# Dilated-window softmax heads on one core: the scores of four heads as one issue unit, values as the stationary operand in column halves, output kept feature-major

## The chip, the cores and the metric

The kernel runs on one core of one Trainium2 chip. The metric is the device time of one execution in microseconds (us), a median over runs; lower is better. The two engines that this document mostly speaks of are TensorE (rows named PE for its matmuls, PEld for the loads of its stationary operand) and the engines that feed it: VectorE (DVE), ScalarE (ACT) and the DMA queue of SyncE (SP).

## The reference

A two-layer decoder trunk on 512 tokens of 1024 features. Layer 0 mixes tokens with four gated delta-rule heads and eight dilated sliding-window softmax heads, layer 1 with a state-space mixer; each is followed by cross-attention and a feed-forward block. The change touches the eight softmax heads alone. Each of three branches attends, from query t, the keys t, t-r, t-2r, ... back to t-window, and the branches are weighted by their log-sum-exp:

```python
SW_BRANCHES = ((128, 1), (512, 4), (2048, 16))
...
    scores = jnp.einsum('brnqhd,brnkhd->brnhqk', qb, kw,
                        preferred_element_type=jnp.float32) * (d ** -0.5)
...
    p = jnp.exp(scores - m)
    l = p.sum(-1)
    o = jnp.einsum('brnhqk,brnkhd->brnqhd', p, vw.astype(jnp.float32))
    o = o / jnp.swapaxes(l, -1, -2)[..., None]
...
    wts = jax.nn.softmax(jnp.stack(lses), axis=0)[..., None]
    return jnp.sum(jnp.stack(outs) * wts, axis=0)
```

With 512 tokens this is one softmax per query over all earlier keys, with the logarithm of the number of branches that see a key (0 to 3) added to its score. The kernel computes it in that form: an additive mask `attm` holds 8 times that logarithm, or -1e30.

## The kernel before

**An order by recording.** The program does not issue instructions as it is written. Class `Order` records every engine call as an operation (`add`, line 219), gives it an estimated duration (`cost`, line 187), and `order` (line 270) then simulates the engines: each engine takes the first operation in program order whose operands are there and whose buffers are free. `issue` (line 417) emits the result; every instruction therefore carries line 422 in the profile, and groups are told apart by tile names and shapes. Tile names: `ps` is a PSUM bank (8 of them), `t` a 128x512 scratch tile in SBUF (13), `big` a 128x2048 tile (16), `raw`, `hi`, `lo` the weights as fetched and split into two parts of reduced float32, `ident` the identity for transposes.

**Products.** Large projections run as three matmuls in reduced float32 (hi*hi, hi*lo, lo*hi; one matmul record each). The softmax heads use plain float32; there one matmul of the program shows as two records, each with its own weight load.

**The softmax heads** are the end of `mixer0` (lines 986 to 1017). Queries and keys lie feature-major, two heads of 64 features in the 128 partitions of `qkT`, values token-major in `Vt`. For each block `i` of 128 queries and each of 8 heads, with n = (i+1)*128 keys:

1. scores: a matmul of 64 rows (a head's features) by n columns into a bank of its own (line 994); even heads lie in partitions 0 to 63, odd heads in 64 to 127;
2. DVE adds the mask and takes the row maximum (line 997), scales it (998); ACT takes the exponential and its row sums (999);
3. PE transposes the weights, i+1 blocks of 128x128 (line 1000); DVE (even heads) or ACT (odd heads) copies them to SBUF (1002 to 1005);
4. the product with the values (line 1007): i+1 matmuls whose stationary operand is the transposed weights (128 columns) and whose moving operand is 64 columns of `Vt`; the output is token-major, 64 columns of the bank `ov` per head.

After the 8 heads the block is scaled by the reciprocal sums on DVE (1014), transposed by PE to feature-major and split into hi and lo parts by ACT and DVE (`to_mix`, line 885), as the operand of the output projection. After each pair of heads the program draws one step of `fill`, the key projection of the cross-attention (`mem_k`, 256-column products). What follows is that output projection (`mix_out0`, 512-column products): the half of its contraction that reads the delta-rule heads can run before the softmax heads are done, the other half cannot.

Of the kernel before, what the change touches and what calls it, by code (L numbers as in the profile page):

```python
# [12 lines left out]
AF = mybir.ActivationFunctionType  # L13
OP = mybir.AluOpType
AX = mybir.AxisListType

P = 128
# [75 lines left out]
class Engine:  # L93
    """Records the calls of an engine instead of issuing them."""
# [10 lines left out]
class Order:  # L105
    """The order in which the recorded instructions are issued: for each engine, the first in program
    order of those whose operands are there, by estimates of what the instructions take."""
# [12 lines left out]
    def either(self, *calls):  # L120
        """The same result by one of several engines: (engine, function, args, kwargs)"""
        self.add(list(calls))

# [6 lines left out]
    # ---- what an access touches  # L130
# [40 lines left out]
    @staticmethod  # L171
    def operands(fn, args, kw):
# [14 lines left out]
    def cost(self, eng, fn, outs, ins, kw):  # L187
        o = outs[0]
        n = 1
        for _, c in list(o.ap)[1:]:  # L190
            n *= c
        psum = any("PSUM" in str(x.space) for x in ins)
# [25 lines left out]
    # ---- recording  # L218
# [50 lines left out]
    # ---- ordering  # L269
# [147 lines left out]
    def issue(self):  # L417
        seq, prio = self.ops, [op.prio for op in self.ops]
        self.issued = self.order(seq, prio)
        with self.tc.manual_schedule():  # L420
            for op, (e, fn, args, kw, _) in self.issued:
                op.inst = getattr(self.eng[e], fn)(*args, **kw)  # L422
# [21 lines left out]
class Trunk:  # L444
# [32 lines left out]
    def weights(self, w, k0, n, c0, width):  # L477
        """n row tiles of w by `width` columns as high and low parts, fetched ahead of the program"""
# [93 lines left out]
    def transposes(self, src, n, width=P):  # L572
        """n blocks of [128, width] from src to one bank [width, n, 128]"""
# [9 lines left out]
    def mixer0(self, fill):  # L583
# [6 lines left out]
        # ---- x, transposed  # L590
# [14 lines left out]
        # ---- constants  # L605
# [19 lines left out]
        # ---- rotary tables  # L625
# [14 lines left out]
        # ---- beta and decay logits, feature-major then token-major  # L640
# [57 lines left out]
        # ---- delta-net q, k, v  # L698
# [44 lines left out]
        # ---- the decay inside a chunk, [j, (head, i)]  # L743
# [24 lines left out]
        # ---- chunk matrices, [j, (head, i)]: L^T above its diagonal  # L768
# [25 lines left out]
        # ---- q and v  # L794
# [3 lines left out]
        # ---- inverse of the 32 x 32 diagonal blocks, one system a partition (h, c, b)  # L798
# [17 lines left out]
        # ---- the products of q and k under the decay  # L816
# [12 lines left out]
        # ---- the gate of the delta-net heads  # L829
# [8 lines left out]
        # ---- merge the blocks: X' = X - X E X for 32, 64  # L838
# [41 lines left out]
        # ---- sequential part over chunks  # L880
# [80 lines left out]
        # ---- the sliding-window heads  # L961
# [24 lines left out]
        off = 0  # L986
        for i in range(NT):
# [3 lines left out]
            for h in range(8):  # L991
                rs = slice(64 * (h % 2), 64 * (h % 2) + 64)
                sp = self.bank()
                T.matmul(sp[:, :n], qkT[0][rs, h // 2, i * P:(i + 1) * P], qkT[1][rs, h // 2, :n], start=True, stop=True)
                pm = t2()
                mx = tiny(1)
                V.tensor_tensor_reduce(pm[:, :n], sp[:, :n], attm[:, off:off + n], 1.0, NEG, OP.add, OP.max, mx)
                V.tensor_scalar(mx, mx, -0.125, None, op0=OP.mult)
# [10 lines left out]
                if h % 2:  # L1009
                    next(fill, None)  # L1010
# [657 lines left out]
```

## Time and profile before

| | |
|---|---|
| median of 3 runs | 1574.64 us |
| lowest and highest run | 1571.55, 1580.14 us |
| span of the profiled execution | 1572.0 us |
| PE busy | 1539.2 us, 98% of the span |
| PEld busy | 1300.8 us, 83% |
| DVE busy | 990.3 us, 63% |
| ACT busy | 550.9 us, 35% |
| DMA | 184.06 MB, mean 117 GB/s |

The profiled execution has no separate time of its own besides its span of 1572.0 us, which lies between the lowest and the median run; nothing measurable lies around it. The softmax heads take the stretch from about 235 to 316 us, with the key projection and the output projection mixed into it. The mean granted clock of TensorE over the span is 0.994. In the rows, "busy" is the union of the records' intervals; matmul records are pipelined and overlap, so a duration of a matmul record is longer than what it costs. What a piece of PE work costs is read from the distance between the starts of two pieces.

### The profile page before, as it was taken

The numbers are of one execution on the slowest core, as the hardware profiler recorded it, in microseconds if no ns is written. First come the engines' busy times: TensorE is split into PE (matmuls) and PEld (weight loads), VectorE is DVE, ScalarE is ACT, GpSimd is POOL, SyncE is SP. The second block draws the span as 40 slices with busy tenths as digits, with TensorE's granted clock in tenths as the row PEclk, the third lists the DMA queues.
The fourth block names the chain that finished last, engine by engine and source line by source line (L and its number), as shares of the span: only waits on it lengthen the run. The fifth ranks groups of instructions, "written<-read, shape, count | busy, mean of one in ns | idle before, by whom it ended". The sixth has DMA issues, their size and how long they took to land.

```text
span 1572.0 us, 20938 instructions
## 1 busy us (share of the span) xinstructions
PE 1539.2 (98%) x8132; PEld 1300.8 (83%) x8132; DVE 990.3 (63%) x1890; ACT 550.9 (35%) x988; POOL 58.2 (4%) x97
## 2 busy tenths in 40 slices
PE   7999999999999999999999899999999999999998
PEld 5887878778988888888888798888888888888886
DVE  6989666556557788725754899748657443334436
ACT  6533436424432344423441233332422322222211
POOL 1100000000000000010000000000000000000000
PEclk9999999999999999999999999999999999999999
DMA  6423224125314344526572554323213333233322
GB/s 184 125 60 95 81 89 134 51 71 168 91 37 132 111 166 163 183 84 201 188 254 81 201 176 148 125 94 108 88 37 98 107 102 100 73 115 96 105 68 94
DMA packets 125539, 184.06 MB, mean 117 GB/s; under 512 B 14144, under 2 KB 84800, under 8 KB 121344
## 3 DMA queue, kind: packets, MB, share of 16 engines
q1 hardware_dynamic: 125440, 182.73, 36.0%
q8 instruction: 64, 1.05, 0.3%
q14 instruction: 35, 0.29, 0.1%
HBM read 162.52 MB, written 20.19 MB: 116 GB/s over the span
## 4 chain that ended last, share of the span: by engine, by line
PE 83%; DVE 10%; DMA 2%; ACT 2%; issue 1%; SPq 0%; POOL 0%; DVEq 0%; ACTq 0%; POOLq 0%
PE ps L422 83%; DVE t L422 5%; DVE big L422 3%; DVE lo L422 2%; ACT big L422 1%; ACT hi L422 1%; DVE tiny L422 1%; DMA raw<-in_xv_w_dram 1%; DMA t<-in_x_t_dram 1%; DMA raw<-in_xo_w_dram 0%; DMA raw<-in_hyb_w_in_dram 0%; ACT L422 0%; DMA raw<-in_hyb_w_out_dram 0%; ACT t L422 0%; DMA prm<-in_dn_a_log_dram 0%
## 5 line engine op out<-in xcount | busy, mean ns | idle before, releaser
L422 PE MATMUL ps<-big,hi 128*128 128x512 f32 (+1 forms) x2368 | 651.4, 361 | 6.4 <-ACT hi L422 4.9
L422 PE MATMUL ps<-hi,big 128*128 128x512 f32 x1728 | 548.1, 395 | 1.1 <-DVE big L422 0.7
L422 PEld LDWEIGHTS ps<-big,hi 128*128 128x128 f32 x2368 | 422.1, 191 | 70.0 <-ACT hi L422 5.3
L422 DVE TENSOR_TENSOR lo<-raw,hi 128x1024 fp32r<-128x1024 f32 (+2 forms) x252 | 303.5, 1205 | 222.8 <-ACT hi L422 220.1
L422 ACT ACTIVATE hi<-raw 128x1024 fp32r<-128x1024 f32 (+2 forms) x252 | 263.5, 1046 | 512.2 <-PE ps L422 356.4
L422 PE MATMUL ps<-big,lo 128*128 128x512 f32 (+1 forms) x1184 | 426.7, 362 | 2.7 <-DVE lo L422 2.6
L422 PEld LDWEIGHTS ps<-hi,big 128*128 128x128 f32 x1728 | 323.2, 188 | 66.5 <-DVE big L422 1.6
L422 PE MATMUL ps<-lo,big 128*128 128x512 f32 x864 | 339.1, 394 | 4.6 <-DVE lo L422 4.5
L422 PEld LDWEIGHTS ps<-big,lo 128*128 128x128 f32 x1184 | 225.5, 191 | 34.8 <-DVE lo L422 3.8
L422 PEld LDWEIGHTS ps<-lo,big 128*128 128x128 f32 x864 | 162.8, 188 | 40.3 <-DVE lo L422 8.0
L422 ACT ACTIVATE big<-ps 128x256 fp32r<-128x256 f32 (+2 forms) x196 | 93.9, 514 | 223.2 <-PE ps L422 214.2
L422 DVE TENSOR_TENSOR big<-ps,big 128x256 fp32r<-128x256 f32 (+1 forms) x160 | 82.2, 545 | 63.0 <-ACT big L422 61.1
L422 ACT ACTIVATE t<-ps 128x512 f32<-128x512 f32 (+4 forms) x129 | 64.5, 510 | 161.9 <-PE ps L422 157.9
L422 DVE SCALAR_TENSOR_TENSOR big<-big,ps 128x512 f32<-128x512 f32 x56 | 38.3, 685 | 95.4 <-PE ps L422 95.4
L422 DVE SCALAR_TENSOR_TENSOR t<-t,ps 128x512 f32<-128x512 f32 x72 | 48.9, 681 | 58.5 <-ACT t L422 53.5
L422 PE MATMUL ps<-big,big 128*128 128x256 f32 (+6 forms) x392 | 72.3, 340 | 0.1
L422 ACT ACTIVATE big<-t 32x128 f32<-32x128 f32 (+1 forms) x140 | 59.9, 443 | 30.6 <-DVE t L422 13.2
L422 PEld LDWEIGHTS ps<-big,t 128*128 128x128 f32 (+2 forms) x496 | 59.4, 186 | 10.8 <-issue 3.6
L422 PE MATMUL ps<-big,t 128*128 128x128 f32 (+3 forms) x496 | 65.5, 276 | 1.8 <-DVE t L422 1.7
L422 DVE SCALAR_TENSOR_TENSOR big<-big,tiny,t 128x512 f32<-128x512 f32 x96 | 66.6, 744 | 0.0
L422 PE MATMUL ps<-ident,t 128*128 128x128 f32 x336 | 60.2, 274 | 3.7 <-ACT t L422 1.9
L422 PEld LDWEIGHTS ps<-big,big 128*128 128x128 f32 (+1 forms) x392 | 54.2, 189 | 8.6 <-issue 1.9
(140 smaller groups left out, 927.7 us busy)
## 6 DMA issues: line engine op xcount, KB each, us to landing
raw<-in_ffn_wg_dram SPq DMA_DIRECT2D x44, 512.0 KB, 3.5
raw<-in_ffn_wu_dram SPq DMA_DIRECT2D x44, 512.0 KB, 3.5
raw<-in_ffn_wd_dram SPq DMA_DIRECT2D x44, 512.0 KB, 3.9
s5m<-big SPq DMA_DIRECT2D x16, 1024.0 KB, 4.4
big<-s5m SPq DMA_DIRECT2D x16, 1024.0 KB, 5.2
raw<-in_hyb_w_in_dram SPq DMA_DIRECT2D x26, 512.0 KB, 3.9
raw<-in_xk_w_dram SPq DMA_DIRECT2D x16, 512.0 KB, 4.9
raw<-in_xv_w_dram SPq DMA_DIRECT2D x16, 512.0 KB, 3.8
```

Of the source, the lines that this page charges most:

```text
L422: op.inst = getattr(self.eng[e], fn)(*args, **kw)
```

## The change

It touches five things, all for the softmax heads.

- `Order.together` records several matmuls as one operation with a given cost, so that they are issued one behind the other; `operands`, `cost` and `issue` know of it.
- The scores of four heads are one such unit, into four banks.
- The product with the values is turned round: 64 columns of `Vt` (one head) are the stationary operand, the transposed weights (128 queries) the moving one. The two heads of a pair write partitions 0 to 63 and 64 to 127 of the same 128 columns of `ov`; the matmuls of a pair are one unit, alternating between the two halves. The output is feature-major.
- The reciprocal sums, needed along the free axis now, are spread to 512 columns by ACT, transposed by PE (4 blocks), copied by ACT to SBUF, and multiplied into `ov` by DVE.
- The four transposes of the output are gone; `split` reads the scaled block from SBUF.

Comments and docstrings are dropped from the file as well, so that line numbers move (422 is 439 for single operations, 437 for those of a unit).

```diff
+    def together(self, cost, calls):
+        self.add([("pe", "together", [("matmul", a, k) for a, k in calls], {"cost": cost})])
...
+        if fn == "together":
+            outs, ins = [], []
+            for c in args:
+                o, i = cls.operands(*c)
+                outs += o
+                ins += i
+            return outs, ins
...
+        if fn == "together":
+            return kw["cost"]
...
+                if fn == "together":
+                    for f, a, k in args:
+                        op.inst = getattr(self.eng[e], f)(*a, **k)
+                    continue
...
-            for h in range(8):
-                rs = slice(64 * (h % 2), 64 * (h % 2) + 64)
-                sp = self.bank()
-                T.matmul(sp[:, :n], qkT[0][rs, h // 2, i * P:(i + 1) * P], qkT[1][rs, h // 2, :n], start=True, stop=True)
...
-                for k in range(i + 1):
-                    T.matmul(ov[:, h * 64:(h + 1) * 64], pt[:, k * P:(k + 1) * P], Vt[:, k, h * 64:(h + 1) * 64],
-                             start=(k == 0), stop=(k == i))
-                if h % 2:
+            for hq in range(2):
+                sps = [self.bank() for _ in range(4)]
+                rs = [slice(64 * (u % 2), 64 * (u % 2) + 64) for u in range(4)]
+                self.o.together(0.00125 * n + 0.3, [
+                    ((sps[u][:, :n], qkT[0][rs[u], hq * 2 + u // 2, i * P:(i + 1) * P], qkT[1][rs[u], hq * 2 + u // 2, :n]),
+                     dict(start=True, stop=True)) for u in range(4)])
+                for hp in range(hq * 2, hq * 2 + 2):
+                    pts = []
+                    for u in range(2):
+                        h, sp = hp * 2 + u, sps[(hp % 2) * 2 + u]
...
+                        pts.append(pt)
+                    self.o.together(0.23 * (i + 1) + 0.1, [
+                        ((ov[u * 64:(u + 1) * 64, hsl(hp)], Vt[:, k, (hp * 2 + u) * 64:(hp * 2 + u + 1) * 64],
+                          pts[u][:, k * P:(k + 1) * P]), dict(start=(k == 0), stop=(k == i)))
+                        for k in range(i + 1) for u in range(2)])
                     next(fill, None)
             V.reciprocal(ls, ls)
+            lw8 = t2()
+            A.activation(lw8.rearrange("p (h c) -> p h c", h=8), ls[:, :, None].to_broadcast([P, 8, 64]), AF.Copy)
+            rl = self.transposes(lambda k: lw8[:, hsl(k)], 4)
             ob = t2()
-            V.tensor_tensor(ob.rearrange("p (h c) -> p h c", h=8), ov.rearrange("p (h c) -> p h c", h=8),
-                            ls[:, :, None].to_broadcast([P, 8, 64]), op=OP.mult)
-            self.dump("mixed", ob, i, 512)
-            to_mix(1, i, ob)
+            A.activation(ob, rl, AF.Copy)
+            V.tensor_tensor(ob, ov, ob, op=OP.mult)
+            cs = slice(i * 32, (i + 1) * 32)
+            for u in range(2):
+                v = mixv[2 + u]
+                self.split(v[:, :, 0, cs], v[:, :, 1, cs],
+                           ob[:, u * 256:(u + 1) * 256].rearrange("p (k c q) -> p k c q", k=2, q=4))
```

**How it moves instructions.** The order on PE, first piece, before: end of the third query block (i = 2) and start of the fourth (i = 3, 512 keys). `big_433,big_432` are keys and queries (a score), `big_415` is `Vt` (product with the values), `ident_72` marks transposes; x3 or x4 is that many in a row.

```order
L422 MATMUL ps_660<-big_433,big_432 128x512
L422 MATMUL ps_614<-big_415,t_574_650 128x64 x3
L422 MATMUL ps_614<-big_415,t_579_655 128x64 x3
L422 MATMUL ps_665<-big_433,big_432 128x512
L422 MATMUL ps_670<-big_433,big_432 128x512
L422 MATMUL ps_657<-ident_72,t_580_656 128x128 x4
L422 MATMUL ps_663<-ident_72,t_585_661 128x128 x4
L422 MATMUL ps_675<-big_433,big_432 128x512
L422 MATMUL ps_668<-ident_72,t_590_666 128x128 x2
L422 MATMUL ps_658<-big_415,t_588_664 128x64 x4
```

The same place in the changed kernel; `ps_718<-..,big_361` is the output projection.

```order
L437 MATMUL ps_616<-t_577_653,big_415 64x128
L437 MATMUL ps_616<-t_581_657,big_415 64x128
L437 MATMUL ps_663<-big_433,big_432 128x512
L437 MATMUL ps_664<-big_433,big_432 128x512
L437 MATMUL ps_665<-big_433,big_432 128x512
L437 MATMUL ps_666<-big_433,big_432 128x512
L439 MATMUL ps_718<-lo_725,big_361 128x512
L439 MATMUL ps_718<-hi_724,big_361 128x512
L439 MATMUL ps_669<-ident_72,t_591_667 128x128 x4
L439 MATMUL ps_673<-ident_72,t_595_671 128x128 x4
```

Before, the eight scores of the fourth block stand in six places, four of them alone and two as neighbouring pairs; now in two places of four. Over all four blocks 17 places become 8: of the 32 heads 10 (six of the third block, four of the fourth) stood without the other head of a pair beside them.

The second piece is the end of the heads on PE, before: last product with the values, then products of the output projection that do not need the heads (`big_360`, `big_361`), the transposes of the heads' output (`ps_701`), and the first product that needs it (`big_362`).

```order
L422 MATMUL ps_658<-big_415,t_623_699 128x64 x4
L422 MATMUL ps_713<-hi_720,big_361 128x512
L422 MATMUL ps_713<-lo_721,big_361 128x512
L422 MATMUL ps_713<-hi_720,big_361 128x512 x2
L422 MATMUL ps_713<-lo_721,big_361 128x512
L422 MATMUL ps_701<-ident_72,t_624_700 128x128 x4
L422 MATMUL ps_713<-hi_720,big_361 128x512
L422 MATMUL ps_714<-hi_717,big_360 128x512
L422 MATMUL ps_714<-lo_718,big_360 128x512
L422 MATMUL ps_714<-hi_717,big_360 128x512
L422 MATMUL ps_712<-hi_723,big_362 128x512
```

The same end in the changed kernel; the first two rows end the last unit of products with the values.

```order
L437 MATMUL ps_661<-t_622_698,big_415 64x128
L437 MATMUL ps_661<-t_626_702,big_415 64x128
L439 MATMUL ps_736<-hi_741,big_360 128x512
L439 MATMUL ps_736<-lo_742,big_360 128x512
L439 MATMUL ps_736<-hi_741,big_360 128x512 x2
L439 MATMUL ps_736<-lo_742,big_360 128x512
L439 MATMUL ps_736<-hi_741,big_360 128x512
L439 MATMUL ps_736<-hi_744,big_361 128x512
L439 MATMUL ps_736<-lo_745,big_361 128x512
L439 MATMUL ps_736<-hi_744,big_361 128x512 x2
L439 MATMUL ps_736<-lo_745,big_361 128x512
L439 MATMUL ps_716<-hi_727,big_362 128x512
```

No transposes stand behind the last product any more (those of the reciprocal sums stand ahead of its unit); behind it come eleven products of the output projection's second half, and then the first that needs the heads. The output projection as a whole starts earlier in the heads: its first product stands in the second query block instead of the fourth.

## Rows read from the trace of the kernel before

**Rows 1.** Page, busy time by engine, and shares of the chain that ended last.
```profile
PE 1539.2 (98%) x8132; PEld 1300.8 (83%) x8132; DVE 990.3 (63%) x1890; ACT 550.9 (35%) x988; POOL 58.2 (4%) x97
...
PE 83%; DVE 10%; DMA 2%; ACT 2%; issue 1%; SPq 0%; POOL 0%; DVEq 0%; ACTq 0%; POOLq 0%
```
**Rows 2.** Windows, stretches of the heads: us, busy (x) of PE, PEld, DVE, ACT, POOL, PEclk.
```profile
244.90:251.90 7.00, 7.00 (x59) 6.75 (x58) 3.96 (x11) 3.74 (x9) 0.00 (x0) 1.00 0.48 153
...
269.40:288.30 18.90, 18.03 (x116) 12.87 (x116) 14.60 (x56) 12.65 (x38) 0.00 (x0) 1.00 0.20 61
288.30:304.30 16.00, 16.00 (x96) 10.52 (x96) 9.03 (x26) 7.28 (x17) 0.00 (x0) 1.00 0.22 64
304.30:316.00 11.70, 11.34 (x69) 9.43 (x68) 3.98 (x11) 3.81 (x8) 0.00 (x0) 1.00 0.13 43
sum 80.80, PE 78.38 PEld 63.32 DVE 49.04 ACT 43.57 POOL 0.00; mean PE 11.20 PEld 9.05 DVE 7.01 ACT 6.22 POOL 0.00
```
**Rows 3.** Timeline of PE, 512 keys: start us, us, engine, line, operation, tiles, xcount.
```profile
288.34 1.12 PE L422 MATMUL ps<-big,big 64*128 64x512 f32 x2
289.39 1.55 PE L422 MATMUL ps<-big,t 128*128 128x64 f32 x12
290.87 1.13 PE L422 MATMUL ps<-big,big 64*128 64x512 f32 x4
291.93 1.09 PE L422 MATMUL ps<-ident,t 128*128 128x128 f32 x8
```
**Rows 4.** Timeline of PE, 128 keys: four heads together, then two, with what follows.
```profile
235.56 0.72 PE L422 MATMUL ps<-big,big 64*128 64x128 f32 x8
236.20 0.50 PE L422 MATMUL ps<-big,hi 128*128 128x256 f32 x2
...
244.93 0.49 PE L422 MATMUL ps<-big,big 64*128 64x128 f32 x4
245.35 0.50 PE L422 MATMUL ps<-big,hi 128*128 128x256 f32 x2
```
**Rows 5.** Timeline of PE: a long run of products with the values.
```profile
281.69 2.12 PE L422 MATMUL ps<-big,t 128*128 128x64 f32 x18
283.64 0.83 PE L422 MATMUL ps<-ident,t 128*128 128x128 f32 x6
```
**Rows 6.** Lines by form, 235.5 to 315.7 us: all products with the values, all 512-key scores.
```profile
L422 PE MATMUL ps<-big,t 128*128 128x64 f32 x160 | 21.0, 271 | 0.0
...
L422 PE MATMUL ps<-big,big 64*128 64x512 f32 x16 | 6.7, 641 | 0.0
```
**Rows 7.** Timeline of PE in the delta-rule stage: two streams in opposite quarters of the array.
```profile
157.02 0.22 PE L422 MATMUL ps<-big,t 64*64 64x64 f32 x1
157.08 0.22 PE L422 MATMUL ps<-t,big 64*64 64x64 f32 x1
157.08 0.22 PE L422 MATMUL ps<-big,t 64*64 64x64 f32 x1
157.13 0.22 PE L422 MATMUL ps<-t,big 64*64 64x64 f32 x1
```
**Rows 8.** Lines by form, same stretch as rows 6: DVE and ACT work per head.
```profile
L422 ACT ACTIVATE t<-t,tiny 128x512 f32<-128x512 f32 x8 | 5.7, 715 | 7.8 <-DVE tiny L422 7.8
L422 DVE CUSTOM_DVE_ANT_0 t<-ps,big 128x512 f32<-128x512 f32 x8 | 5.5, 688 | 6.7 <-PE ps L422 6.7
L422 DVE TENSOR_SCALAR tiny<-tiny 128x1 f32<-128x1 f32 x32 | 4.6, 149 | 0.5
L422 DVE COPY t<-ps 128x512 f32<-128x512 f32 x4 | 2.7, 685 | 0.6 <-PE ps L422 0.6
L422 ACT ACTIVATE t<-ps 128x512 f32<-128x512 f32 x4 | 2.4, 598 | 4.6 <-PE ps L422 4.6
```
**Rows 9.** Timeline of PE: the longest waits in the third block and at the end.
```profile
270.88 0.44 PE L422 MATMUL ps<-ident,t 128*128 128x128 f32 x2 [0.54 <-ACT t L422]
...
272.39 0.44 PE L422 MATMUL ps<-ident,t 128*128 128x128 f32 x2 [0.23 <-ACT t L422]
...
315.72 0.73 PE L422 MATMUL ps<-hi,big 128*128 128x512 f32 x2 [0.36 <-DVE big L422]
```

More of the change, by code (lines that the diff above doesn't have):

```diff
@@ L169, in covers, with operands @@
         return (a[0] <= b[0] and b[1] <= a[1]) if isinstance(a, tuple) else not (b & ~a)
-    @staticmethod
-    def operands(fn, args, kw):
+    @classmethod
+    def operands(cls, fn, args, kw):
+        if fn == "together":
[5 more added lines that the diff above has]
+            return outs, ins
         isap = lambda x: hasattr(x, "ap") and hasattr(x, "tensor")
@@ L983, in mixer0, with rows @@
         self.gemm_tok(w_in, 0, KT, 2056, actt, NT, rope_sink(0), tail=TAIL)
-        off = 0
-        for i in range(NT):
+        def rows(i, off):
             n = (i + 1) * P
@@ L990, in mixer0 @@
             ls = tiny(8)
-            for h in range(8):
-                rs = slice(64 * (h % 2), 64 * (h % 2) + 64)
-                sp = self.bank()
-                T.matmul(sp[:, :n], qkT[0][rs, h // 2, i * P:(i + 1) * P], qkT[1][rs, h // 2, :n], start=True, stop=True)
[L995 to L998, printed above, removed]
-                A.activation(pm[:, :n], pm[:, :n], AF.Exp, bias=mx, scale=0.125, accum_out=ls[:, h:h + 1])
-                tp = self.transposes(lambda k: pm[:, k * P:(k + 1) * P], i + 1)
-                pt = t2()
-                if h % 2:
-                    A.activation(pt[:, :n], tp[:, :n], AF.Copy)
-                else:
-                    V.tensor_copy(pt[:, :n], tp[:, :n])
-                for k in range(i + 1):
-                    T.matmul(ov[:, h * 64:(h + 1) * 64], pt[:, k * P:(k + 1) * P], Vt[:, k, h * 64:(h + 1) * 64],
-                             start=(k == 0), stop=(k == i))
-                if h % 2:
+            for hq in range(2):
[8 more added lines that the diff above has]
+                        h, sp = hp * 2 + u, sps[(hp % 2) * 2 + u]
+                        pm = t2()
+                        mx = tiny(1)
+                        V.tensor_tensor_reduce(pm[:, :n], sp[:, :n], attm[:, off:off + n], 1.0, NEG, OP.add, OP.max, mx)
+                        V.tensor_scalar(mx, mx, -0.125, None, op0=OP.mult)
+                        A.activation(pm[:, :n], pm[:, :n], AF.Exp, bias=mx, scale=0.125, accum_out=ls[:, h:h + 1])
+                        tp = self.transposes(lambda k: pm[:, k * P:(k + 1) * P], i + 1)
+                        pt = t2()
+                        if u:
+                            A.activation(pt[:, :n], tp[:, :n], AF.Copy)
+                        else:
+                            V.tensor_copy(pt[:, :n], tp[:, :n])
+                        pts.append(pt)
[3 more added lines that the diff above has]
+                        for k in range(i + 1) for u in range(2)])
@@ L1010, in mixer0 @@
                     next(fill, None)
-            off += n
             V.reciprocal(ls, ls)
+            lw8 = t2()
+            A.activation(lw8.rearrange("p (h c) -> p h c", h=8), ls[:, :, None].to_broadcast([P, 8, 64]), AF.Copy)
+            rl = self.transposes(lambda k: lw8[:, hsl(k)], 4)
             ob = t2()
-            V.tensor_tensor(ob.rearrange("p (h c) -> p h c", h=8), ov.rearrange("p (h c) -> p h c", h=8),
-                            ls[:, :, None].to_broadcast([P, 8, 64]), op=OP.mult)
@@ L1016, in mixer0 @@
-            self.dump("mixed", ob, i, 512)
-            to_mix(1, i, ob)
+            A.activation(ob, rl, AF.Copy)
[5 more added lines that the diff above has]
+                           ob[:, u * 256:(u + 1) * 256].rearrange("p (k c q) -> p k c q", k=2, q=4))
+        off = 0
+        for i in range(NT):
+            rows(i, off)
+            off += (i + 1) * P
```

## The prediction, made before the changed kernel ran

> **What bounds the kernel now.** I read the page first: PE is busy for 1539.2 of 1572.0 us, and 83% of the chain that ended last is PE work [rows 1], so PE work that goes away should shorten the whole, unless PE then waits. Next the windows over the softmax heads: in 80.80 us PE is busy for 78.38, with the granted clock at 1.00 (the level of 2.4 GHz), while DVE has 49.04 and ACT 43.57 [rows 2]. So the stretch is a queue on PE with 2.4 us of waits. What a piece of PE work costs there comes from the distances of starts in the timeline [rows 3 to 5], its amount from the lines by form [rows 6], what the other engines need per head from [rows 8], and where PE waited from [rows 9]. The sum is made against the profiled 1572.0 us; the median of the runs lies 2.6 us higher.
>
> **Scores.** One head of 512 keys alone takes from 288.34 to 289.39, 1.05 us; a group of two heads from 290.87 to 291.93, 1.06 [rows 3]. The two heads of a pair lie in different row halves of the array, and the second one is free. With 128 keys four heads take 0.64 us (235.56 to 236.20), two take 0.42 (244.93 to 245.35) [rows 4]: every further pair costs 0.22 us at 128 keys, hence 0.44, 0.66 and 0.88 at 256, 384 and 512, as the streams are that much longer. What is left, 0.18 to 0.20 us, is a fixed cost inside a group. There is one outside as well: 18 product records take 1.95 us to the next piece, 0.109 each [rows 5], but the 12 between two groups of scores take 1.48 [rows 3], 0.17 more than 12 x 0.109. Leaving the full-array arrangement and coming back thus costs 0.37 us a group.
>
> Before, the order has the scores in 17 groups. The sixteen heads of the first two blocks all stand in pairs; of the third block six heads stand alone beside one pair, of the fourth four alone beside two pairs. That is 17 x 0.37 = 6.3, and 4 x 0.22 + 4 x 0.44 + 7 x 0.66 + 6 x 0.88 = 12.5, in all 18.8 us. After, it is 8 groups of two pairs: 8 x 0.37 + 4 x (0.22 + 0.44 + 0.66 + 0.88) = 3.0 + 8.8 = 11.8. **Scores save 7.0 us.** Every price in this term has its row.
>
> **Values.** Before, 160 records [rows 6] at 0.109 are 17.4 us. Such a record streams only 64 columns and is paced by its load of 128 columns. After, it is still 160 records; each loads 64 columns and streams 128, and a stream of 128 columns costs 0.11 (half of the 0.22 above, two records a matmul). What no row of before shows is whether two matmuls in the two column halves, over the same 128 rows, run side by side. Bounds: fully, 80 x 0.11 = 8.8 us; not at all, 17.6. The nearest rows are the two streams of 64x64 matmuls in opposite quarters, which interleave with each stream keeping its own step of 0.06 [rows 7], and the score pairs; both lie in different rows too, so they speak for the overlap without showing it. I take the full overlap, 8.8, and keep 17.6 for the range.
>
> The trace speaks against a load waiting for the stream on its own rows: the product records of before fill all rows, and at 0.109 a record [rows 5] there is no room for a load of 128 columns plus a stream of 64 one behind the other (0.11 + 0.055). A rule of the Trainium skill (TensorE: Matmul & The Clock Gate, "Part 3: Packing small matmuls — row/col tiling", its list of what overlaps) says otherwise: weight loads overlap with matmuls in flight only where the row group differs. By that rule the halves would load and stream in turn; this case's trace does not bear it out for the full array, and no row shows column halves. It is a rival below.
>
> The 16 units of products now leave the full arrangement too. The scores' 0.37 is the upper bound, with a load of 128 columns at the head of a group; with 64 columns, half of that 0.11 goes, so 0.31. I take 0.32: 5.1 us, less 3 x 0.17 where a unit touches a unit of scores in the order and shares the way out, 4.6. **Values cost 13.4 instead of 17.4, saving 4.0 us**; by the upper bound 3.2.
>
> **Sums, scaling, transposes.** Four transposes a block go and four come: nothing on PE. ACT gets two 512-column operations a block, 0.6 us each [rows 8], 4.8 us in all, beside 43.57 busy of 80.80 [rows 2]. If that cover went, in the fourth block, a pair of heads needs on DVE 2 x (0.69 + 0.15) + 0.69 = 2.4 us, on ACT 2 x 0.72 + 0.60 = 2.0 plus the row sums' reading [rows 8], while PE still needs a share of scores of 1.07, eight transposes of 0.11 and a unit of 0.32 + 0.88, together 3.1. PE stays the bound, by half a microsecond or so a pair, with output-projection products between. DMA: five issues on SP change places, none is added.
>
> **Waits.** PE waits 0.54 and 0.23 us at 270.88 and 272.39 for the exponentials of the third block, and 0.36 at 315.72 for the heads' output [rows 9]. In the new order products of the output projection stand in the third block, and behind the last values eleven of them cover a chain (scaling, split) from which four transposes are gone. I count these 1.1 us as gained. Bounds: 0, if other waits take their place, and 2.4, if all go. What is late next is the first exponential of the first block, on which the order changes little.
>
> **Sum.** 7.0 + 4.0 + 1.1 = 12.1 us of 1572.0: a span of 1559.9, and with the 2.6 us that the median stood above the span **1562.5 us**.
>
> **The rivals.**
> - *Heads become latency-bound.* Four scores are issued before the first exponential, the unit is costed for the scheduler at less than the 2.1 us it will take at 512 keys, and PE finishes its part sooner. For it: DVE already has 14.60 of 18.90 us in the third block [rows 2]. Against: it had 9.03 of 16.00 in the fourth, and the products of the projection fill. If each of the eight pairs in the last two blocks waits 0.6 us, 4.8 of the gain is lost: 1567.
> - *The column halves run in turn*, loads hidden. Then the values cost 17.6 + 4.6 = 22.2, 4.8 more than before instead of 4.0 less: 1562.5 + 8.8 = 1571.3. For it: no row shows two streams over the same rows. Against: [rows 7].
> - *Halves in turn, and each load waits for the stream on its rows.* Each record costs 0.11 + 0.055: 160 x 0.165 = 26.4, 17.6 more than forecast: 1580.1, 5.5 us slower than before, 0.35%. This is what the skill's rule would make; [rows 5] speak against it.
> - *Changing between the halves drains the array*, as going to and from the row halves does. The price outside a group is 0.17 us; paid by each of 80 matmuls it is 13.6 on top of the halves in turn: 1584.9, slower than before by 0.65%. It decides from (1574.6 - 1571.3) / 80 = 0.04 us a change on. For it: the score groups pay it at each border. Against: the two streams of quarters change with every record at no cost [rows 7].
> - *The change does not do what it says*: the order shows that it does, for the issue; the second rival is what remains of this.
>
> **How the numbers follow.** Forecast 0.70, latency-bound heads 0.09, halves in turn 0.11, with waiting loads 0.05, drained 0.05. The forecast's own range is 1558 to 1567 (waits -1.3 to +1.1, border price 0.8, and the runs of before, which lie from 1571.55 to 1580.14, for the rest). The range of 8 in 10 takes in the first two rivals: 1557 to 1572. A measurement of this kernel can tell about 0.5%, 7.9 us, from no change: below 1566.8 is faster, above 1582.5 slower. Faster: nearly all of the forecast and half of the first rival, 0.71. Slower: the last rival and part of the one before, 0.07. Same: 0.22.
>
> **What would show it.** Scores: eight groups of 64-row records, each four heads at 512 keys in about 2.0 us. Values: records of 128 columns on 64 in nearly simultaneous pairs, a unit of the fourth block in about 1.2 us; twice that, or records 0.11 apart one by one, means halves in turn; 0.165 apart means waiting loads. Waits: PE's in the last two blocks below 1 us in all; more, and released by ACT or DVE, is the first rival. The forecast is wrong if the stretch of the heads, up to the first output-projection product that needs them, shrinks by less than 8 us, or if it shrinks and the time is given back behind it.

## The result, and the profile after

The changed kernel takes 1559.76 us (median of 5 runs, 1559.38 to 1563.14), beside 1573.37 for the kernel before in the same comparison. The ratio is 0.9911, 95% interval 0.9884 to 0.9938: 13.6 us less, and by the interval 9.8 to 18.3. The gain is under 2%, but clear of no change. The forecast was 1562.5, with a range from 1557 to 1572. The profiled execution has a span of 1557.9 us and a time of its own of 1559.76. Every run on record lies 1.7 to 1.9 us above its span like this one; so something does lie around the span of before too, and about 1.8 of the 2.6 us that its median stood above its span is not spread between runs.

The page of the changed kernel, busy time by engine and the shares of the chain, which answer to [rows 1]:

```profile
PE 1523.2 (98%) x8132; PEld 1285.8 (83%) x8132; DVE 989.4 (64%) x1890; ACT 555.2 (36%) x996; POOL 57.6 (4%) x97
...
PE 84%; DVE 10%; DMA 2%; ACT 2%; issue 1%; SPq 0%; POOL 0%; DVEq 0%; ACTq 0%; POOLq 0%
```

The number of matmul records is the same as before, and PE is busy for 16.0 us less, part of which is clock and not work, as shown below. PE is still what the end waits for, so the time follows. The windows over the heads of the changed kernel, to be laid beside [rows 2] (columns: us, busy (x) of PE, PEld, DVE, ACT, POOL, then PEclk):

```profile
...
267.40:290.10 22.70, 22.70 (x172) 15.77 (x170) 15.04 (x52) 15.53 (x41) 0.00 (x0) 1.00 0.25 84
290.10:294.00 3.90, 2.80 (x14) 0.98 (x10) 3.29 (x9) 1.79 (x4) 0.00 (x0) 1.00 0.00 0
294.00:299.50 5.50, 4.76 (x16) 2.31 (x16) 2.73 (x11) 2.87 (x9) 0.00 (x0) 0.69 0.00 0
299.50:312.60 13.10, 13.10 (x117) 10.51 (x116) 7.84 (x18) 8.62 (x17) 0.00 (x0) 1.00 0.42 117
sum 78.10, PE 75.09 PEld 58.41 DVE 50.34 ACT 49.09 POOL 0.00; mean PE 10.73 PEld 8.34 DVE 7.19 ACT 7.01 POOL 0.00
```

PE's idle time in these windows did not shrink: it is 78.10 - 75.09 = 3.0 us, where it was 2.4. So the gain must be work that PE no longer has. The third block (first row) now has no wait at all; the beginning of the fourth (second and third row) has one, and a stretch in which the granted clock is 0.69. The timeline of PE there (start us, us, engine, line, operation, tiles, xcount, in brackets the wait and who ended it) shows the new units, the wait and the clock in one piece:

```profile
290.25 1.99 PE L437 MATMUL ps<-big,big 64*128 64x512 f32 x8
292.16 0.50 PE L439 MATMUL ps<-lo,big 128*128 128x512 f32 x1
292.50 0.40 PE L439 MATMUL ps<-hi,big 128*128 128x512 f32 x1
294.17 0.66 PE L439 MATMUL ps<-ident,t 128*128 128x128 f32 x4 [1.28 <-ACT t L439]
295.39 1.11 PE L439 MATMUL ps<-ident,t 128*128 128x128 f32 x4 [0.57 <-ACT t L439]
296.43 3.17 PE L437 MATMUL ps<-big,big 64*128 64x512 f32 x8
299.53 0.66 PE L439 MATMUL ps<-ident,t 128*128 128x128 f32 x4
300.12 1.09 PE L437 MATMUL ps<-t,big 128*64 128x128 f32 x16
301.14 0.66 PE L439 MATMUL ps<-ident,t 128*128 128x128 f32 x4
```

Read by starts: four heads of 512 keys take 1.91 us (290.25 to 292.16; the forecast said about 2.0). The same unit takes 3.10 at 296.43, where the clock is down. A unit of values takes 1.02 us (300.12 to 301.14; forecast about 1.2). Inside it the records of the two column halves start 6 to 7 ns apart and the pairs 0.109 apart, so the halves do run side by side, and going from one to the other and back costs nothing.

**Where the time went.** The profile lets the same record be found in each trace by counting PE's matmul records back from the last one; this is a surer ruler than the clock time, since what lies ahead of the heads varies from run to run (below). From the 6960th record before the last, ahead of the heads ("entry"), to the 6060th, in the cross-attention, is the heads' stretch. The table gives it, and inside it the distances from each record to the next, summed by kind (us). A wait inside a group of scores or right behind it is in the column of the scores.

| profile | entry at | heads' stretch | scores | values | entry to end |
|---|---|---|---|---|---|
| before | 226.1 | 156.5 | 16.8 | 17.0 | 1345.9 |
| changed kernel | 225.4 | 145.3 | 11.4 | 11.2 | 1332.5 |
| changed kernel again (e8) | 227.0 | 145.4 | 11.4 | 11.2 | 1332.8 |
| scores alone (e1) | 229.1 | 151.0 | 11.7 | 16.9 | 1340.0 |
| values alone (e2) | 228.5 | 151.0 | 17.8 | 11.2 | 1338.2 |
| halves grouped (e3) | 231.4 | 146.8 | 10.2 | 14.2 | 1334.6 |
| both costs raised (e4) | 227.4 | 144.3 | 10.2 | 11.2 | 1330.5 |
| one half (e6) | 225.8 | 151.9 | 10.2 | 19.8 | 1340.9 |
| values by four heads (e7) | 226.8 | 150.3 | 12.1 | 10.0 | 1338.4 |
| score cost alone (e9) | 227.8 | 143.4 | 10.2 | 11.4 | 1330.6 |

The heads' stretch is 11.2 us shorter. Another 2.6 us of the profiled difference is no work of the heads: the same 28 records near 890 to 905 us ran at half clock (1.2 GHz) in the profile of before and at full clock (2.4 GHz) in that of the changed kernel, after a wait of 2.06 us that both have. Seven of the fourteen profiles have such a stretch there, costing 1.1 to 2.6 us (before, e1, e3, e6, e7, e11, e12); it is in the last column of the table, and not in the heads' stretch. First before, then the changed kernel:

```profile
902.70:908.70 6.00, 5.95 (x28) 5.95 (x29) 6.00 (x10) 1.06 (x1) 0.10 (x1) 0.50 0.66 224
```
```profile
890.50:893.90 3.40, 3.33 (x28) 3.33 (x29) 3.40 (x7) 0.06 (x1) 0.00 (x0) 1.00 0.61 183
```

### The profile page after: what moved, and what is told of

It reads as the page before. It is cut to its first block, busy times and chain, and to the rows that moved or that the text cites. A ratio compares the mean times of both kernels' runs of the same rounds, so it can differ in the third digit from the quotient of the medians.

```text
span 1557.9 us, 20944 instructions
## 1 busy us (share of the span) xinstructions
PE 1523.2 (98%) x8132; PEld 1285.8 (83%) x8132; DVE 989.4 (64%) x1890; ACT 555.2 (36%) x996; POOL 57.6 (4%) x97
## 4 chain that ended last, share of the span: by engine, by line
PE 84%; DVE 10%; DMA 2%; ACT 2%; issue 1%; SPq 0%; POOL 0%; DVEq 0%; ACTq 0%; POOLq 0%
PE ps L439 83%; DVE t L439 5%; DVE big L439 2%; DVE lo L439 2%; PE ps L437 1%; DMA raw<-in_xo_w_dram 1%; ACT big L439 1%; DVE tiny L439 1%; ACT hi L439 1%; DMA big<-s5m 0%; ACT L439 0%; DMA t<-in_x_t_dram 0%; DMA raw<-in_xv_w_dram 0%; DMA raw<-in_hyb_w_in_dram 0%; DMA prm<-in_dn_a_log_dram 0%
## 5 line engine op out<-in xcount | busy, mean ns | idle before, releaser
L439 ACT ACTIVATE big<-ps 128x256 fp32r<-128x256 f32 (+2 forms) x188 | 89.6, 508 | 205.8 <-PE ps L439 196.9
L439 DVE TENSOR_TENSOR big<-ps,big 128x256 fp32r<-128x256 f32 (+1 forms) x152 | 77.5, 541 | 54.6 <-ACT big L439 52.6
L439 ACT ACTIVATE big<-t 32x128 f32<-32x128 f32 (+2 forms) x148 | 64.4, 455 | 32.4 <-DVE t L439 14.2
L439 POOL TENSOR_TENSOR tiny<-tiny,mhalf 128x1 f32<-128x1 f32 (+1 forms) x28 | 23.6, 846 | 965.8 <-DVE tiny L439 965.8
L439 PEld LDWEIGHTS ps<-ident,t 128*128 128x128 f32 x336 | 41.8, 141 | 16.4 <-issue 5.6
L439 PE MATMUL ps<-big,big 128*128 128x256 f32 (+2 forms) x328 | 55.2, 314 | 0.0
L439 DVE TENSOR_TENSOR big<-t,big 128x512 fp32r<-128x512 f32 (+1 forms) x68 | 44.0, 680 | 13.9 <-ACT big L439 13.7
```

## The experiments

**Each part alone (e1, e2).** e1 takes the value products back to the form of before and keeps the four-head scores; e2 keeps the turned values and issues each head's scores by itself.

The edit of e1, then that of e2:

```diff
-                    self.o.together(0.23 * (i + 1) + 0.1, [
...
+                        for k in range(i + 1):
+                            T.matmul(ov[:, h * 64:(h + 1) * 64], pts[u][:, k * P:(k + 1) * P], Vt[:, k, h * 64:(h + 1) * 64],
+                                     start=(k == 0), stop=(k == i))
```
```diff
-                self.o.together(0.00125 * n + 0.3, [
...
+                        T.matmul(sp[:, :n], qkT[0][rs[u], hp, i * P:(i + 1) * P], qkT[1][rs[u], hp, :n], start=True, stop=True)
```

> The change's score units alone: four heads' scores per unit, products with the values and output as before. PE-cost theory (two heads of a pair cost as one, and 17 departures from the full array become 8): the 64-row records take about 10 us in the heads instead of 16.9 between their starts, the borders about 1.5 us less, so 6 to 7.5 us less than before: 1566 to 1567.5, ratio 0.9955. Rival, order theory (the gain comes from other work being moved into the heads, not from cheaper PE work): the whole 13.6 us or none, 1560 or 1573.

> The turned product with the values and the feature-major output alone, scores recorded head by head as before. PE-cost theory: records of the values take 11 us instead of 17, their 16 departures from the full array give back 2 to 3, so 3 to 5 us less than before: 1568.5 to 1570.5. With the scores alone it adds up to the whole change, 10 to 12.5 us without waits. Order theory: the gain of the two parts doesn't add up, one of them alone gives nearly all.

e1 takes 1567.75 us (ratio 0.9953, 0.9934 to 0.9973), e2 1568.55 (0.9955, 0.9934 to 0.9975), beside 1574.1. The heads' stretch is 5.5 us shorter in each, in all 11.0, and 11.2 in the change as a whole. (From entry to end it is 5.9 and 7.7 beside 13.4, but there the low clock of before behind the heads counts, in the sum of the parts twice.) So the two parts add up and each is worth about half; against the order theory, neither alone gives the whole gain. The time of e1 lies just above its range, that of e2 at the lower end of its own. The split is a rough one: the order of e2 has 19 groups of scores where before has 17, so its scores take 17.8 us, and in e1 the low clock of the fourth block is in the 11.7. In e1 the wait of the fourth block is there too, and longer, while in e2 PE's one wait there is 0.27 us. It belongs to the four-head scores. PE in e1:

```profile
297.67 0.40 PE L439 MATMUL ps<-hi,big 128*128 128x512 f32 x1
300.82 0.87 PE L439 MATMUL ps<-ident,t 128*128 128x128 f32 x4 [2.75 <-ACT t L439]
301.61 3.42 PE L437 MATMUL ps<-big,big 64*128 64x512 f32 x8
```

**Do the halves overlap, and what for (e3, e6).** e3 issues all matmuls of one half and then all of the other; e6 does the same, with both heads of a pair in one half.

The edit of e3, then what e6 has besides it (the first operand of the matmul, its output):

```diff
-                        for k in range(i + 1) for u in range(2)])
+                        for u in range(2) for k in range(i + 1)])
```
```diff
-ov[u * 64:(u + 1) * 64, hsl(hp)]
+ov[(hp % 2) * 64:(hp % 2) * 64 + 64, hsl(hp // 2 * 2 + u)]
```

> The changed kernel, but inside each unit all products of the first head stand ahead of those of the second, instead of in alternation; nothing else moves. If the two column halves overlap only when neighbours in the order belong to different halves: 12 units (blocks two to four) lose 0.44, 0.66 and 0.88 us each, 7.9 us in all, 1567.6. If each half of the array works off its own instructions as far as they are queued: no change, 1559.8, and records of the two halves still start in pairs.

> The matmuls of a pair one head behind the other, as in e3_halves_grouped, but both heads of a pair write the same column half (the pairs of a block go to the lower and the upper half by turns), so that every pair of heads lands in another place of the output; the amount of work is unchanged. In e3 a unit of 16 records of the fourth block took 1.51 us, in the changed kernel, which alternates, 1.02. Theory that the column halves run side by side: with one half there is nothing to overlap, a matmul costs its whole stream of 0.218 us, the units take 0.15 + 0.44 us for each block of keys, 0.59, 1.02, 1.46 and 1.90, in all 19.9 us for the sixteen units against 14.2 in e3 and 11.2 in the changed kernel; the heads' stretch is 5 to 6 us longer than e3's 146.8. Rival, that records overlap whatever half they write (a queue of prepared loads): as e3, 1.51 us and 14.2.

e3 takes 1565.79 us (0.9927, 0.9901 to 0.9954); e6, a single run, 1568.42. e6 leaves the heads in other places of the output than the reference has them; its work on PE is the same. The unit of values that follows the second scores of the fourth block, in e3 (first) and in e6:

```profile
303.12 1.99 PE L437 MATMUL ps<-big,big 64*128 64x512 f32 x8
305.04 0.66 PE L439 MATMUL ps<-ident,t 128*128 128x128 f32 x4
305.62 1.58 PE L437 MATMUL ps<-t,big 128*64 128x128 f32 x16
307.13 0.66 PE L439 MATMUL ps<-ident,t 128*128 128x128 f32 x4
```
```profile
303.64 1.96 PE L437 MATMUL ps<-t,big 128*64 128x128 f32 x16
305.53 0.66 PE L439 MATMUL ps<-ident,t 128*128 128x128 f32 x4
```

One half: 1.89 us for 16 records; two halves grouped, 1.51; two halves alternating, 1.02. All values together are 19.8, 14.2 and 11.2 us. The e6 figure had been put at 19.9, and its heads' stretch at 5 to 6 us above e3's (it is 5.1), so it is the different halves that let the records overlap. e3's heads' stretch is 1.5 us longer than the changed kernel's: 3.0 more in the values, less 1.6 of low clock in the fourth block that its profile does not have. The rest of its longer span is its late entry and low clock near 900 us. e3 fell between its two theories, and its trace says why: in the units of two and four records a half the second half's first record starts 7 and 14 ns after the first half's, and the step is that of the alternating order; in the units of six it starts 0.28 us after, when three records of the first half have started, and in the units of eight, as in the one above, 0.49 us after, when five have. Then both run side by side, and the second ends alone. In the units of four, six and eight alike, three records of the first half are still to start: in this order the second half is reached about four records ahead. This is a reading of starts in one order, not a count of a queue.

e6 also bears on the rival with waiting loads: all its records write one half over the same rows, and 16 of them take 1.89 us, of which 0.15 is the unit's fixed cost: 0.109 each, as [rows 5] had it for the full array; stream and load one behind the other would be 16 x 0.165 = 2.64. The list of what overlaps in the Trainium skill (TensorE: Matmul & The Clock Gate, "Part 3: Packing small matmuls — row/col tiling"), by which a load overlaps a matmul in flight only where the row group differs, is not borne out by these traces: all records of e6 use the same 128 rows and start 0.109 us apart.

**The wait of the fourth block (e4, e8, e9, e10).** The scheduler simulates the engines with the costs given to a unit. For the scores of 512 keys it had 0.00125 x 512 + 0.3 = 0.94 us; the trace has 1.92. The edit of e4 is this one; e9 has the first of the two corrections alone, e10 has 0.00334 * n + 0.2 and 0.22 * (i + 1) + 0.2:

```diff
-                self.o.together(0.00125 * n + 0.3, [
+                self.o.together(0.0034 * n + 0.35, [
-                    self.o.together(0.23 * (i + 1) + 0.1, [
+                    self.o.together(0.22 * (i + 1) + 0.3, [
```

> The changed kernel with the durations that its profile shows given to the scheduler for the two kinds of unit (scores 0.0034 n + 0.35 us instead of 0.00125 n + 0.3, values 0.22 (i + 1) + 0.3 instead of 0.23 (i + 1) + 0.1). If the waits of 2.0 us in the fourth block, and the half clock behind them (1.6 us), come from the scheduler's belief that a unit of scores takes half of what it does: both go, 1556. If they come from the chain on VectorE and ScalarE whatever the estimate: within 1 us of 1559.8.

> The changed kernel unaltered, beside the others. The profiled runs entered the heads (the same record of the heads' first stretch) at 225.4 (changed kernel), 226.1 (before), 227.4, 228.5, 229.1 and 231.4 us (experiments), though everything ahead of the heads stands in the same order in the changed kernel and in e3_halves_grouped, the first and the last of these. Theory that this spread belongs to the start of a run (DMA at 89 to 107 GB/s between 20 and 40 us, stretches of half clock) and not to the kernels: the entry lies anywhere from 225 to 231, and the rest, 1332.5 us from the entry to the end, comes again within 1.5 us, the wait and half clock of the fourth block with it. Rival, that the kernels make it: the entry comes again at 225.4 within 0.5 us.

> The changed kernel with only the scheduler's cost of a unit of scores corrected (0.0034 us a key and 0.35, where it had 0.00125 and 0.3: 2.09 us at 512 keys instead of 0.94; the trace has 1.92). Theory that this cost is what puts too few projection products ahead of the transposes of the fourth block: the wait of 1.46 and 0.73 us there falls below 1 us, as in e4_true_costs (0.34 and 0.37), no half clock follows, and from the entry to the heads to the end it takes 1330 to 1331.5, against 1332.5 and 1332.8 in the two profiles of the changed kernel. Rival, that the cost of the units of values did it in e4: the wait stays near 2.2 us and the rest at 1332.5.

> Both costs set to the measured values (scores 0.2 us and 0.00334 a key, values 0.2 and 0.22 a block of keys), a little below those of e4_true_costs. Theory that the waits come from wrong costs: waits of PE in the fourth block below 1 us and none of e4's 1.2 us at the first products of the cross-attention by the same reason, so from the entry to the heads to the end 1329 to 1331, the best of all, and a time of 1557 to 1560. Rival, that waits are set by the chain scores, exponential, transposes, whatever the costs say, and come up elsewhere: 1331 to 1333.

e4 takes 1560.94 us (0.9907, 0.9873 to 0.9941), the changed kernel again 1561.34 (0.9901, 0.988 to 0.9923), e9 1560.83 (0.9926, 0.9911 to 0.9941), e10 1562.73 (0.994, 0.9923 to 0.9956). By times none can be told from the changed kernel; the 1556 of e4 and the 1557 to 1560 of e10 were not reached. The traces tell more. In e8 the wait and the low clock of the fourth block come again, and the rest from the entry on within 0.3 us, while the entry itself moved by 1.6: that much of the spread comes with the same kernel. From entry to end e4, e9 and e10 take 1330.5, 1330.6 and 1330.8, 2 us less. Most of this is clock: without the 1.6 us of low clock in the fourth block the heads' stretch of the changed kernel would be 143.7, and in e4, e9 and e10 it is 144.3, 143.4 and 143.9. The same place in e9, without a wait:

```profile
286.33 1.99 PE L437 MATMUL ps<-big,big 64*128 64x512 f32 x8
288.25 0.55 PE L439 MATMUL ps<-ident,t 128*128 128x128 f32 x3
288.55 0.48 PE L439 MATMUL ps<-hi,big 128*128 128x512 f32 x1
288.86 0.38 PE L439 MATMUL ps<-ident,t 128*128 128x128 f32 x2
289.18 1.07 PE L437 MATMUL ps<-t,big 128*64 128x128 f32 x12
290.18 1.63 PE L439 MATMUL ps<-ident,t 128*128 128x128 f32 x9
```

With the true cost the scheduler puts values and transposes of the third block behind the scores of the fourth, and they cover its first exponentials. The score cost alone does it (e9). But waits came up elsewhere: behind the heads one of 0.5 us in e9, in e10 two of 0.22 and 0.53, for splits of weights on DVE, in e4 two of 0.5, for DVE and ACT, where the changed kernel has none. The expectation that they would go with the exact costs is wrong. And since e3 and e6 kept the two waits of the fourth block without the low clock, it is not shown that taking the wait away is what kept the clock up in these three.

**Is it DVE's work at the end of a block (e11, e12)?** In the changed kernel DVE has, in front of the transposes that wait:

```profile
290.45 0.69 DVE L439 TENSOR_TENSOR t<-ps,t 128x512 f32<-128x512 f32 x1 [3.00 <-PE ps L437]
291.41 0.69 DVE L439 CUSTOM_DVE_ANT_0 t<-ps,big 128x512 f32<-128x512 f32 x1 [0.27 <-PE ps L437]
...
292.02 1.12 DVE L439 TENSOR_TENSOR big<-t,big 128x256 fp32r<-128x256 f32 x2
293.06 0.15 DVE L439 TENSOR_SCALAR tiny<-tiny 128x1 f32<-128x1 f32 x1
293.12 0.69 DVE L439 CUSTOM_DVE_ANT_0 t<-ps,big 128x512 f32<-128x512 f32 x1
```

The splits of the third block's output (third row) stand between the first mask and its scaling. e11 records the end of a block behind the softmax of the next block's first pair; e12 does so with the score cost of e9.

```diff
-            V.reciprocal(ls, ls)
...
+            def tail():
+                V.reciprocal(ls, ls)
...
+                    if hp == 0 and prev:
+                        prev()
```

> The changed kernel with the end of a block (reciprocal sums, their transposes, scaling, splits) recorded after the softmax of the next block's first pair, so that DVE takes the mask and maximum of the new block first; costs as in the changed kernel. In the changed kernel DVE had the scaling (0.69 us) and two splits (1.12 us) of the third block in front of or between the first mask and its scaling of the fourth, and PE, with two products left, waited 1.28 and 0.57 us. Theory that those DVE operations make the wait: no wait of PE over 0.5 us in the fourth block, no half clock there, and 1330 to 1331.5 us from the entry to the heads to the end. Rival, that the chain of a four-head unit is too long whatever DVE has in front: the wait stays at 1 us or more (in all) in the fourth block, since now both units of scores stand ahead of every transpose, and the rest takes 1332 or more.

> As e11_tail_later, with the corrected cost of a unit of scores of e9_score_cost_only. e9 had no wait in the fourth block and 1330.6 us from the entry to the heads to the end. If the splits on DVE are all that was left, both remedies together are no better than one, 1330 to 1331; if they add up, 1328.5 to 1329.5 and a time of 1556 to 1559, faster than the changed kernel. Rival: the later end of a block delays the projection products that need it or brings new waits, 1331.5 or more.

e11 takes 1563.7 us (0.9936, 0.9915 to 0.9957), e12 1562.5 (0.9924, 0.9904 to 0.9945); from entry to end 1334.8 and 1333.3. The heads' stretch is 146.0 and 145.2, longer than the 143.4 of e9, though the granted clock stays up in both. The theory falls: the wait is still there, 1.22 us, for a copy that DVE does later (1.24 in e12, for another result of DVE).

```profile
294.83 2.78 PE L437 MATMUL ps<-big,big 64*128 64x512 f32 x8
297.53 0.66 PE L439 MATMUL ps<-ident,t 128*128 128x128 f32 x4
299.41 1.81 PE L439 MATMUL ps<-ident,t 128*128 128x128 f32 x10 [1.22 <-DVE t L439]
```
```profile
297.54 1.13 DVE L439 TENSOR_TENSOR big<-t,big 128x256 fp32r<-128x256 f32 x2 [0.39 <-ACT big L439]
298.58 0.69 DVE L439 COPY t<-ps 128x512 f32<-128x512 f32 x1
```

First PE in e11, then DVE: the splits have only moved in front of the next thing that PE needs. What takes the wait away is other work on PE behind the scores, as in e9. This order also put both units of scores ahead of every transpose of their exponentials, so the part of DVE alone is not isolated.

**Fewer borders (e7, e7c).** The values of four heads as one unit: 8 units instead of 16. The score cost is that of e4 in e7 and 0.0034 * n + 0.2 in e7c, which also has 0.2 for the 0.3 below.

```diff
-                    self.o.together(0.23 * (i + 1) + 0.1, [
...
-                        for k in range(i + 1) for u in range(2)])
-                    next(fill, None)
+                self.o.together(0.44 * (i + 1) + 0.3, [
...
+                    for hp in range(hq * 2, hq * 2 + 2) for k in range(i + 1) for u in range(2)])
+                next(fill, None)
+                next(fill, None)
```

> The products with the values of four heads as one unit (8 units instead of 16), and the scheduler's costs of both kinds of unit set to what the traces show. In the changed kernel a unit costs 0.151 us besides its 0.218 a pair of matmuls, and 0.09 ahead of it: 0.245 a border. Theory that what counts is PE's work at borders: 8 x 0.245 = 2.0 us less than e4_true_costs from the entry to the heads to the end (1330.6), that is 1328.5 and a time near 1558. Rival, latency: all four heads must be through exponentials, transposes and copies before the unit may start, PE waits 0.5 us or more at each of the four units of the last two blocks, and the time is that of e4, 1561, or above.

> As e7_value_quads, but with the costs of both kinds of unit a little lower (0.2 us instead of 0.35 and 0.3 besides the streams), which moves key-projection products out of the gap between the second and third block and one or two projection products elsewhere. Border theory: the same work, so from the entry to the heads to the end within 1 us of e7_value_quads. Rival, that the time hangs on where the fill products stand: waits of PE of over 1 us appear or go in one of the two, and they differ by as much.

e7 takes 1568.98 us (0.9947, 0.9925 to 0.9969), e7c 1567.32 (0.9939, 0.9917 to 0.9961), slower than the changed kernel, which takes 1561.34 in the same comparison (e8). The borders did save: values take 10.0 us instead of 11.2, and with about 1 us on the way into and out of the eight units that are gone this is the 2.0 that was expected. The rival took it back several times over, first of all in the first block, where both units of scores now stand side by side and little covers the exponentials. From entry to end e7 takes 1338.4 and e7c 1339.5, 1.1 us apart where the border theory had at most 1; both have these waits, and behind them the granted clock is at half for a while (from 245.7 us in e7), which it is not at that place in the changed kernel. PE in e7:

```profile
237.86 0.71 PE L437 MATMUL ps<-big,big 64*128 64x128 f32 x8
238.91 0.66 PE L439 MATMUL ps<-ident,t 128*128 128x128 f32 x4 [0.34 <-DVE tiny L439]
240.47 0.33 PE L439 MATMUL ps<-ident,t 128*128 128x128 f32 x1 [0.90 <-ACT t L439]
241.27 0.30 PE L439 MATMUL ps<-ident,t 128*128 128x128 f32 x1 [0.47 <-DVE t L439]
```

## Why the prediction was right

- **Scores, 7.0 foreseen, 7.2 measured.** Eight units, as said; a unit of four heads takes 0.65, 1.06, 1.49 and 1.92 us from 128 to 512 keys, that is 0.22 and 0.43 for each 128 keys (foreseen 0.2 and 0.44). The 16.8 us of before hold 0.9 of waits, those of the third block; without them the scores took 15.9, and without the low clock, as in e3, they take 10.2. By starts the way into a group costs 0.09 to 0.10 and the way out 0.06 to 0.08, together the 0.17 that was foreseen; nine groups are gone, 1.5.
- **Values, 4.0 foreseen, 4.2 measured.** The choice of full overlap was right, and with it the price of one pair, 0.109. A unit costs 0.15 besides its pairs and about 0.16 on the way in and out, the 0.32 that was taken. With 11.2 inside the units and 2.4 at their borders the values cost 13.6 (foreseen 13.4). Before, they cost 17.0 by starts, and 17.8 with what they cost the first record behind them (foreseen 17.4).
- **Halves in turn**, the rival put 8.8 us higher: e6 makes it by construction, and its values take 8.6 us more than those of the changed kernel. The rival with a drain at each change between the halves needed 0.04 us a change to decide; the records 6 to 7 ns apart and pairs at 0.109 leave no room for it.
- **Waits, 1.1 foreseen: this step failed.** The two waits of the third block and the one at the end, which were counted as gained, are gone. But the text named the first block as what is late next, and looked at the fourth only pair by pair ("PE stays the bound, by half a microsecond or so a pair"). The first pair behind a four-head unit has no earlier pair to cover it; the order showed just two products between the scores of 512 keys and the transposes. There PE waits 1.28 and 0.57 us, and the granted clock falls behind that, which costs another 1.2 in the scores and 0.4 in four transposes (1.04 us from 295.39, where e3 has 0.59). The wait of the first block, which the order was said to change little, grew from 0.82 to 1.17 us. By distances of starts, counting what is over 0.25 us beyond the usual one between two such records, the heads' stretch had 4.2 us of waits at eight places before and has 3.5 at three now, 0.7 less, of which 1.2 are three waits behind the heads that no one had counted; the low clock takes 1.6. The term came to -0.9 instead of +1.1, below its lower bound of 0.
- **The sum.** 7.2 + 4.2 - 0.9 = 10.5, and the heads' stretch is 11.2 us shorter, for 12.1 foreseen. The other 0.7 was in no term: it lies in distances of before that are each less than 0.25 us over the usual one, most of them around 512-column products, and why stays open. So the sum came within 0.9 of the measured shortening with one term off by 2.0, partly by luck.
- **Latency-bound heads**: the rival happened at one of the eight pairs of the last two blocks, with 2.2 us of wait by starts where it had put down 0.6 for a pair, and 1.6 of low clock behind it.
- **The comparison with the median.** The time came out 2.7 us below the forecast although the heads gave 0.9 less than foreseen. The sum was made against a profile of before that held 2.6 us of low clock near 900 us. The two profiled spans differ by 14.1: 11.2 in the heads, 2.2 behind them, where that clock is, and 0.7 ahead of them. The measured ratio allows 9.8 to 18.3 us; the traces of the heads say 11.2. What the medians show beyond that is not explained by the change.

## What to carry to other kernels

A matmul of 64 columns leaves half the array free; a second one beside it in the other column half came free here (0.109 us a pair of records, as for one), if the two were issued alternately. Units of several matmuls save the way into and out of such an arrangement, but they also move the first result of the next stage later: look behind each unit for the work that covers the first chain. The unit's measured cost, given to the scheduler, put such work there, but brought no gain in time that can be told from the spread. Compare traces from the same record on, when what lies ahead varies by more than the effect.

## What the runs showed of the hardware

- **Overlap of column halves depends on the order of issue.** Alternating, plain float32 matmuls over the same rows in two halves take 0.109 us a pair of records; grouped by eight records a half, a unit takes 1.51 us instead of 1.02; in one half, 1.89. In the grouped order records of the second half start while three of the first half are still to start.
- **The granted clock after a wait is not settled by the wait.** With the same order outside the units of values and the same two waits of the fourth block it fell to half in the profiles of the changed kernel and e8, and stayed up in e3 and e6 (the scores behind it take 3.1 us or 1.92). The waits near 890 us show the same: half clock in before, none in the changed kernel. So a profile can lose 1 to 3 us by it at either place and the next one not; what decides it stays open.
- **The start of a run varies, and most of it goes with the granted clock.** Two programs alike up to the heads (the changed kernel and e3) entered them at 225.4 and 231.4 us. Ahead of that the changed kernel has no stretch at half clock, e3 has 13.7 us, which can cost up to half as much, 6.8; e8, the changed kernel again, has 3.4 us and entered 1.6 later, and e6, with none, entered at 225.8. In the window from 40 to 60 us PE is busy throughout in both, in e3 (first, granted clock 0.89) with fewer records than in the changed kernel (1.00):

```profile
40.00:60.00 20.00, 20.00 (x118) 17.67 (x117) 15.35 (x52) 11.99 (x37) 3.04 (x3) 0.89 0.35 97
```
```profile
40.00:60.00 20.00, 20.00 (x134) 18.04 (x133) 18.03 (x59) 11.85 (x31) 3.04 (x3) 1.00 0.37 105
```

Between 20 and 40 us e3 moved 89 GB/s and the changed kernel 107; which of the two, clock or transfers, led to the other is not shown.
